# What a convolution tap is queued behind: the last but one stick product named, instead of the last finished attention piece

## The chip, the cores and the metric

The kernel runs on one core of one Trainium2 chip. A core has a tensor engine (PE, with its weight loads listed apart as PEld), a vector engine (DVE), a scalar engine (ACT), GpSimd (POOL) and a queue engine that issues transfers (SP). Each works through its own list of instructions in order, and they wait for one another through semaphores. The metric is the device time of one execution in microseconds; the kernel before took 2762.03 us (median of 3 runs, 2759.02 to 2770.19).

## What is computed

One step of a two-layer encoder, 1024 prompt tokens and 8 x 16 sample tokens (1152 in all), width 1024, in float32. Layer 0 runs two mixers side by side on one projection: stick-breaking attention (8 heads of 64) and a depthwise convolution of 31 taps over 512 channels. Layer 1 is a band attention. Each layer ends with a squared-ReLU MLP.

```python
def stick_breaking(q, k, v, q_pos, k_pos):
    z = jnp.einsum('bqhd,bkhd->bhqk', q, k).astype(jnp.float32) * (HEAD_DIM ** -0.5)
    mask = k_pos[None, :] < q_pos[:, None]
    log_keep = jnp.where(mask, jax.nn.log_sigmoid(-z), 0.0)
    between = lax.cumsum(log_keep, axis=3, reverse=True) - log_keep
    w = jnp.where(mask, jnp.exp(jax.nn.log_sigmoid(z) + between), 0.0)
    return jnp.einsum('bhqk,bkhd->bqhd', w.astype(v.dtype), v)
...
def conv_module(u_ext, dw_w, dw_b, ln_g, ln_b):
    y = lax.conv_general_dilated(
        u_ext, dw_w[:, None, :], window_strides=(1,), padding='VALID',
        dimension_numbers=('NWC', 'WIO', 'NWC'), feature_group_count=CONV_CH) + dw_b
    return jax.nn.silu(layernorm(y, ln_g, ln_b))
```

## The kernel before

**Stages.** Layer 0's mixer fills about the first 560 us of the trace, the rest is its MLP, layer 1 and its MLP. The mixer handles four head pairs p = 0 to 3, one after another. While the attention of pair p runs, the tensor engine also computes the projections of pair p + 1 (`psp`), the convolution's gate and value for later channels (`psg`, `psa`), and the sample attention (`zs`, `so`).

**Attention of a pair.** For each head i (0, 1) and each block t of 256 queries, the two query tiles q = 2t and 2t + 1 go through `one(q)`: scores `z` on PE (L926, L927, L929), two sigmoids on ACT into `sg` and `kp` (L930, L931), then `stick` on DVE: a running product along the keys (the scan, L909) and the product of the sigmoid with it (L911), which writes `sg`, the weights. This last one is the *stick product*. There are 64 of them and 8 for the samples (`sgs`). The weights are turned by PE (`tpa`, L388), copied by ACT (`wa`, L390), multiplied with the values (`ava`, L398), and the two halves are added by DVE at L410 into `cpa`, the finished *attention piece*, of which there are 32. Names carry the pair, the head and the query tile: `sg207` is pair 2, head 0, tile 7.

**Convolution.** The 512 channels are four blocks of 128 (`u0` to `u3`). Each of the 31 taps of a block is two DVE instructions (L734 for the first tap, L737 for the others): 128x1024 elements for the prompt and 128x128 for the samples, added into `y`; the last tap writes back to `u`. The result goes to `cat_d` in DRAM and is read back for the normalisation (`yl`, L1017) while pair 3 runs.

**What sets the order.** The kernel names its instructions in one program order: lists of steps are merged by planned tensor time, and the taps are spread between them by planned vector time (`level`). A scheduler of the framework then orders each engine's own list by what it expects to be ready. A tap depends on little, so it could be placed far ahead of the attention's vector work. L731 holds it back: `tc.issue_after(x)` orders what is named in the block behind instruction x in x's engine list. It adds no semaphore, as both are on DVE. `prior` holds x, and while it is empty (before the first piece) the taps are free.

## Time and profile before

| | |
|---|---|
| median of 3 runs | 2762.03 us (2759.02 to 2770.19) |
| the profiled execution | 2761.51 us, of which the span of its instructions is 2759.7 us |
| instructions in the profile | 50582 |
| DVE taps (L734, L737) | 248, the last starts at 409.7 us |
| stick products (L911) | 72, from 108.6 us to 537.7 us |

The page's first part gives each engine's busy time; a view by windows gives the same for chosen stretches with the granted tensor clock; the view of waits sums what an engine stood idle for, by the instruction that released it; the timeline lists instructions with their start, their duration and, in brackets, the idle time ahead of them and who ended it. All times are counted from the start of the span. DVE instructions overlap slightly at their ends, so what one costs its queue is the distance from its start to the next start.

### The profile page before, as it was taken

Reading aid. Unit: us, or ns where it says so; the run is one execution under the profiler, and the core shown is the slowest. Engines: PE = TensorE matmul, PEld = TensorE weight load, DVE = VectorE, ACT = ScalarE, POOL = GpSimd, SP = SyncE. Lnnn points to the kernel's source line nnn. Section 1 sums busy time; section 2 is a strip of 40 time slices with the busy share of each in tenths; the row PEclk is TensorE's granted clock in tenths of the full one; section 3 lists DMA queues with packets and bytes.
Section 4 is the critical chain, followed back from the end, with each engine's and each line's share of the span. In section 5 each row is a group of like instructions: output and inputs, shape, how many; then the busy total and the mean of one; then the engine's idle time right before and its main releaser. Section 6 shows DMA issues by size and latency. Waiting matters only on the chain.

```text
span 2759.7 us, 50582 instructions
## 1 busy us (share of the span) xinstructions
PE 2681.8 (97%) x19362; PEld 2556.6 (93%) x19362; DVE 2093.9 (76%) x4117; ACT 1388.9 (50%) x2906; POOL 329.4 (12%) x599
## 2 busy tenths in 40 slices
PE   8999998999999999999999999998999999999998
PEld 8987775799999999999999999997999999999998
DVE  8999997888777755758577777778787777647577
ACT  5344456755555543435355555556555555434344
POOL 1000101041111100000011111110221111100001
PEclk9999998999999999999999999999999999999999
DMA  4434446454343377435444444446533343674344
GB/s 157 125 107 145 128 144 201 149 168 139 137 144 142 141 266 248 123 103 167 148 138 139 140 137 133 138 133 222 184 130 137 140 144 139 237 256 136 98 124 144
DMA packets 173203, 422.90 MB, mean 153 GB/s; under 512 B 25968, under 2 KB 53808, under 8 KB 170912
## 3 DMA queue, kind: packets, MB, share of 16 engines
q1 hardware_dynamic: 135696, 288.38, 33.3%
q0 software_dynamic: 37120, 131.27, 13.9%
q8 instruction: 152, 2.49, 0.4%
q14 instruction: 91, 0.75, 0.1%
q10 hardware_dynamic: 144, 0.02, 0.0%
HBM read 289.60 MB, written 117.34 MB: 147 GB/s over the span
## 4 chain that ended last, share of the span: by engine, by line
PE 82%; DVE 10%; ACT 3%; DMA 2%; issue 2%; SPq 0%; DVEq 0%; ACTq 0%; POOLq 0%
PE pd L1692 25%; PE um L1463 25%; PE psc L225 10%; PE psp L225 5%; PE avc L469 2%; PE psoa L225 2%; PE tpc L457 2%; DVE y L737 1%; DVE kp L909 1%; PE f L225 1%; PE zs L570 1%; PE zc L1203 1%; PE psob L225 1%; PE zc L1204 1%; PE ava L398 1%
## 5 line engine op out<-in xcount | busy, mean ns | idle before, releaser
L225 PE MATMUL psc<-h,hl_wc 128*128 128x384 f32 x1728 | 327.2, 339 | 0.0
L225 PEld LDWEIGHTS psc<-h,hl_wc 128*128 128x128 f32 x1728 | 296.8, 188 | 13.3 <-issue 10.9
L1463 PE MATMUL um<-sl,hl_m 128*128 128x288 f32 x1548 | 241.7, 297 | 0.0
L1463 PEld LDWEIGHTS um<-sl,hl_m 128*128 128x128 f32 x1548 | 219.2, 190 | 0.0
L1692 PE MATMUL pd<-tm,hl_wd 128*128 128x288 f32 x1584 | 214.7, 294 | 0.0
L1692 PEld LDWEIGHTS pd<-tm,hl_wd 128*128 128x128 f32 x1584 | 211.2, 189 | 0.0
L737 DVE SCALAR_TENSOR_TENSOR y<-u,dw,y 128x1024 f32<-128x1024 f32 (+1 forms) x232 | 177.5, 807 | 0.5
L225 PE MATMUL psp<-h,hl_wi 128*128 128x384 f32 x864 | 165.2, 343 | 0.0
L1470 ACT ACTIVATE hdm<-hdm 128x288 f32<-128x288 f32 x192 | 84.7, 442 | 156.5 <-DVE hdm L1469 154.9
L225 PEld LDWEIGHTS psp<-h,hl_wi 128*128 128x128 f32 x864 | 149.8, 190 | 7.6 <-issue 7.2
L186 DVE TENSOR_TENSOR tm<-xr,tm 128x576 fp32r<-128x576 f32 (+1 forms) x120 | 85.9, 716 | 93.1 <-ACT tm L185 93.0
L185 ACT ACTIVATE tm<-xr 128x576 fp32r<-128x576 f32 (+1 forms) x120 | 77.6, 647 | 94.4 <-PE pd L1692 76.2
L1463 PE MATMUL um<-sl,hl 128*128 128x288 f32 x756 | 119.1, 296 | 0.0
L1170 ACT ACTIVATE s<-s,mxc 128x640 f32<-128x640 f32 (+4 forms) x128 | 88.8, 694 | 59.6 <-DVE mxc L1167 58.0
L1692 PE MATMUL pd<-th,hl_wd 128*128 128x288 f32 x792 | 113.9, 297 | 3.7 <-DVE th L186 3.5
L1692 PEld LDWEIGHTS pd<-th,hl_wd 128*128 128x128 f32 x792 | 108.4, 190 | 4.6 <-DVE th L186 4.0
L1692 PE MATMUL pd<-xr,hl_wd 128*128 128x288 f32 x792 | 112.2, 295 | 0.0
L1692 PEld LDWEIGHTS pd<-xr,hl_wd 128*128 128x128 f32 x792 | 107.8, 189 | 0.0
L1463 PEld LDWEIGHTS um<-sl,hl 128*128 128x128 f32 x756 | 106.4, 188 | 0.8
L1692 PE MATMUL pd<-tm,hl 128*128 128x288 f32 x768 | 104.9, 295 | 0.0
L1692 PEld LDWEIGHTS pd<-tm,hl 128*128 128x128 f32 x768 | 103.1, 188 | 0.0
L185 ACT ACTIVATE whc<-tpc 128x512 fp32r<-128x512 f32 (+1 forms) x144 | 72.4, 523 | 46.5 <-PE tpc L457 45.6
(526 smaller groups left out, 6651.4 us busy)
## 6 DMA issues: line engine op xcount, KB each, us to landing
xr<-hb_d SPq DMA_DIRECT2D x208, 288.0 KB, 3.0
xr<-in_w_up_dram SPq DMA_DIRECT2D x64, 512.0 KB, 4.3
hb_d<-hdm POOLq DMA_DIRECT2D x96, 288.0 KB, 2.4
hb_d<-t POOLq DMA_DIRECT2D x96, 288.0 KB, 2.4
wm<-in_w_down_dram SPq DMA_DIRECT2D x64, 256.0 KB, 4.1
st_wd<-in_w_down_dram SPq DMA_DIRECT2D x64, 256.0 KB, 3.6
st_wc<-in_w_in_c_dram SPq DMA_DIRECT2D x44, 256.0 KB, 2.9
xm_d<-xo POOLq DMA_DIRECT2D x16, 576.0 KB, 3.6
```

The source lines that it names most:

```text
L185: ACT(hi, src, AF.Copy)
L186: return tt(lo, src, f(hi), ALU.subtract)
L225: mm(ps()[:, :G], hl[:, a, at:at + P], act[g][k // 4][b][:, k % 4, :], start=n == 0, stop=n == len(todo) - 1)
L398: mm(st["av"][64 * m:64 * m + 64, o0:o0 + n], vs[:, j, i], st["w"][gi][:, c0:c0 + n], start=gi == 0, stop=gi == last)
L457: nc.tensor.transpose(tp[:, c0 + q * P:c0 + (q + 1) * P], blocks.get(j, tile_q), ident)
L469: mm(st["av"][:, o0:o0 + n], vs[:, j, i].rearrange("p a d -> p (a d)"), src[:, c0:c0 + n], start=st["done"] == 0, stop=st["done"] == nmm - 1)
L570: mm(box["z"][at // 512][own, at % 512:at % 512 + kw], qb[:, own], k[:, b * kw:b * kw + kw], start=True, stop=True)
L737: stt(src if j == CW - 1 else dst, src, wj, dst, ALU.mult, ALU.add)
L1170: ACT(s[:, :n], s[:, :n], AF.Exp, bias=mx, scale=-1.0, accum_out=tot)
L1463: mm(banks[b, n][:, :TQ], w[:, a, c * P:c * P + P], combo(key, c)[:, h, n * TQ:n * TQ + TQ], start=k < 3 and c == 0 and i == 0, stop=c == ...
L1470: ACT(y, y, AF.Relu)
L1692: mm(ps, w[:, a, m * P:m * P + P], b[:, h, (n - ns[0]) * TQ:(n - ns[0]) * TQ + TQ], start=first and s == 0, stop=j == NJ - 1 and s == 2, s ...
```

## The change

A list `sticks` collects every stick product as it is named. After each one, `prior["weights"]` is set to the last but one of them (to the first, while there is only one). `finish` no longer sets it. So a tap stands behind the stick product named before the latest one, and no longer behind the latest finished piece. Taps named before the first stick product are free, as before they were until the first piece.

```diff
@@ -185,7 +185,7 @@
-    prior = {}
+    prior, sticks = {}, []
 
@@ -407,7 +407,7 @@
-            prior["weights"] = tt(piece[own, one:], av[0:64, one:256], tmp[own, one:], ALU.add)
+            tt(piece[own, one:], av[0:64, one:256], tmp[own, one:], ALU.add)
             cat.put(piece, own, t * 256, 256)
 
@@ -908,7 +908,8 @@
                 nc.vector.tensor_tensor_scan(keep[:, 0:n][:, ::-1], keep[:, 0:n][:, ::-1],
                                              ones[:, 0:1].to_broadcast([P, n]), 1.0, ALU.mult, ALU.mult)
-                tt(w[:, 0:n - 1], w[:, 0:n - 1], keep[:, 1:n], ALU.mult)
+                sticks.append(tt(w[:, 0:n - 1], w[:, 0:n - 1], keep[:, 1:n], ALU.mult))
+                prior["weights"] = sticks[-min(len(sticks), 2)]
```

The instructions are the same ones in both programs. Lines behind L910 are counted one higher in the new kernel. On DVE 232 instructions get another rank in the engine's list, 101 of them tap instructions; the last that is moved starts at 411.7 us in the trace of before, and behind it the lists agree. On PE one group of transposes and two matmuls are moved by a few places.

First place, DVE in pair 0, where the convolution's value `u2` is taken out of PSUM (L717), the sample scores are masked (`zn001`) and half a weight chunk is split (`hl_wi11_0`). Before:

```order
L717 TENSOR_TENSOR u2_1415<-psa21_1652,u2_1415 128x384
L737 SCALAR_TENSOR_TENSOR y1_1239<-u1_389,dw_77,y1_1239 128x1024
L953 TENSOR_TENSOR zn001_1720<-zn001_1720,masks_82 128x128
L737 SCALAR_TENSOR_TENSOR y1_1239<-u1_389,dw_77,y1_1239 128x128
L737 SCALAR_TENSOR_TENSOR y1_1239<-u1_389,dw_77,y1_1239 128x1024
L737 SCALAR_TENSOR_TENSOR y1_1239<-u1_389,dw_77,y1_1239 128x128
L186 TENSOR_TENSOR hl_wi11_0_1776<-st_wi11_0_1774,hl_wi11_0_1776 128x512
```

Now:

```order
L717 TENSOR_TENSOR u2_1415<-psa21_1652,u2_1415 128x384
L954 TENSOR_TENSOR zn001_1720<-zn001_1720,masks_82 128x128
L186 TENSOR_TENSOR hl_wi11_0_1776<-st_wi11_0_1774,hl_wi11_0_1776 128x512
L909 SCALAR_TENSOR_TENSOR kp011_1711<-kp011_1711,ones_74 128x256
L911 TENSOR_TENSOR sg011_1710<-sg011_1710,kp011_1711 128x255
L737 SCALAR_TENSOR_TENSOR y1_1239<-u1_389,dw_77,y1_1239 128x1024
L909 SCALAR_TENSOR_TENSOR kps01_1724<-kps01_1724,ones_74 128x1152
```

The four tap instructions (two taps) between `u2` and the split have gone behind the stick product `sg011`.

Second place, DVE at the start of pair 1, around `sg101`. Before:

```order
L909 SCALAR_TENSOR_TENSOR kps10_2450<-kps10_2450,ones_74 128x1152
L186 TENSOR_TENSOR hl_wi14_1_2501<-st_wi14_1_2499,hl_wi14_1_2501 128x512
L911 TENSOR_TENSOR sgs10_2449<-sgs10_2449,kps10_2450 128x1151
L909 SCALAR_TENSOR_TENSOR kp101_2472<-kp101_2472,ones_74 128x256
L737 SCALAR_TENSOR_TENSOR y2_2281<-u2_1415,dw_77,y2_2281 128x1024
L911 TENSOR_TENSOR sg101_2471<-sg101_2471,kp101_2472 128x255
```

Now:

```order
L909 SCALAR_TENSOR_TENSOR kps10_2450<-kps10_2450,ones_74 128x1152
L909 SCALAR_TENSOR_TENSOR kp101_2472<-kp101_2472,ones_74 128x256
L911 TENSOR_TENSOR sgs10_2449<-sgs10_2449,kps10_2450 128x1151
L911 TENSOR_TENSOR sg101_2471<-sg101_2471,kp101_2472 128x255
L186 TENSOR_TENSOR hl_wi14_1_2501<-st_wi14_1_2499,hl_wi14_1_2501 128x512
```

`sg101` has the half tap and the weight split behind it instead of ahead.

Third place, DVE towards the end of pair 2, around `sg207`; `q0` (L353) and `l0` (L351) prepare the queries and keys of pair 3. Before:

```order
L911 TENSOR_TENSOR sgs21_3946<-sgs21_3946,kps21_3947 128x1151
L737 SCALAR_TENSOR_TENSOR y3_3216<-u3_2561,dw_77,y3_3216 128x128
L353 SCALAR_TENSOR_TENSOR q0_741<-sq03_3559,q0_741 64x1024
L909 SCALAR_TENSOR_TENSOR kp207_3974<-kp207_3974,ones_74 128x1024
L640 COPY cs02_4038<-sq020_4036 64x64
L911 TENSOR_TENSOR sg207_3973<-sg207_3973,kp207_3974 128x1023
```

Now:

```order
L911 TENSOR_TENSOR sgs21_3946<-sgs21_3946,kps21_3947 128x1151
L737 SCALAR_TENSOR_TENSOR y3_3216<-u3_2561,dw_77,y3_3216 128x1024
L737 SCALAR_TENSOR_TENSOR y3_3216<-u3_2561,dw_77,y3_3216 128x128
L737 SCALAR_TENSOR_TENSOR y3_3216<-u3_2561,dw_77,y3_3216 128x1024
L909 SCALAR_TENSOR_TENSOR kp207_3974<-kp207_3974,ones_74 128x1024
L737 SCALAR_TENSOR_TENSOR y3_3216<-u3_2561,dw_77,y3_3216 128x128
L911 TENSOR_TENSOR sg207_3973<-sg207_3973,kp207_3974 128x1023
```

The same taps stand ahead of `sg207` in both (some of them nearer to it now), but `q0` and one of the copies have gone behind it, `q0` together with `l0` by some 15 instructions.

## The prediction

> **What bounds the kernel now.** I read the page first, then the mixer by windows, then what the tensor engine waits for there.

> ```profile
> span 2759.7 us, 50582 instructions
> PE 2681.8 (97%) x19362; PEld 2556.6 (93%) x19362; DVE 2093.9 (76%) x4117; ACT 1388.9 (50%) x2906; POOL 329.4 (12%) x599
> ```

> Over the whole span PE is the bound. The windows (PE, PEld, DVE, ACT, POOL, then granted clock) split the mixer where the taps end:

> ```profile
> 150.00:400.00 250.00, 234.95 (x1772) 195.34 (x1772) 244.03 (x326) 119.39 (x279) 24.56 (x43) 0.99 0.44 132
> 400.00:560.00 160.00, 143.22 (x958) 108.43 (x957) 129.82 (x224) 108.75 (x239) 17.07 (x31) 0.94 0.52 169
> ```

> From 150 to 400 us DVE is busy 98% and PE 94%: two nearly full queues that hold each other up. Moving taps inside this stretch takes no work out of it. The one kind of wait that leads PE's list there:

> ```profile
> PE tpa L388 <- DVE sg L911: 12.3, 7, 3.3
> ```

> That is 12.3 of PE's 250 - 234.95 = 15.05 us of idle time: seven times a transpose waits for a stick product; the rest is two waits for `u`. The timeline of PE gives six of the seven (the other, near 279.6, is what is left, 0.9 us) and the longer wait for `u`:

> ```profile
> 155.95 0.55 PE L388 MATMUL tpa<-ident,sg 128*128 128x128 f32 x3 [1.23 <-DVE sg L911]
> ...
> 164.93 2.38 PE L225 MATMUL psa<-h,hl_wi 128*128 128x384 f32 x12 [1.62 <-DVE u L717]
> ...
> 218.41 0.77 PE L388 MATMUL tpa<-ident,sg 128*128 128x128 f32 x5 [3.23 <-DVE sg L911]
> ...
> 244.71 0.41 PE L388 MATMUL tpa<-ident,sg 128*128 128x128 f32 x2 [1.07 <-DVE sg L911]
> ...
> 335.50 0.77 PE L388 MATMUL tpa<-ident,sg 128*128 128x128 f32 x5 [3.29 <-DVE sg L911]
> ...
> 375.00 0.99 PE L388 MATMUL tpa<-ident,sg 128*128 128x128 f32 x7 [0.83 <-DVE sg L911]
> ...
> 391.99 0.98 PE L388 MATMUL tpa<-ident,sg 128*128 128x128 f32 x7 [1.73 <-DVE sg L911]
> ```

> The chain of waits, cut to 100 to 420 us, shows which taps really stand ahead of such a wait:

> ```profile
> 147.60 3.02 DVE y L737 x5
> ...
> 160.03 4.38 DVE y L737 x6
> ...
> 322.45 4.38 DVE y L737 x6
> ```

> These are the taps ahead of the wait at 155.95, of the one at 164.93 and of the longest one, at 335.50. In the new list they stand where they stood. This is why I expect little.

> **The change, part by part.** It adds and removes no instruction, transfer or semaphore; a product comes earlier or later by the sum of what was moved across it. Because DVE hardly idles there, that sum is the shift.

> *Products that are waited for, unmoved.* Ahead of `sg017` (218.41), `sg107` (near 279.6) and `sg117` (335.50) the list holds the same instructions: shift 0, and these waits hold 3.23 + 0.9 + 3.29 = 7.4 of the 12.3 us.

> *A loss of DVE time at the first place.* DVE and, last, ACT in the trace of before:

> ```profile
> 134.97 0.56 DVE L704 TENSOR_TENSOR u<-u,rh 128x384 f32<-128x384 f32 x1 [0.64 <-ACT u L703]
> ...
> 164.33 0.55 DVE L717 TENSOR_TENSOR u<-psa,u 128x384 f32<-128x384 f32 x1
> 164.80 1.27 DVE L737 SCALAR_TENSOR_TENSOR y<-u,dw,y 128x1024 f32<-128x1024 f32 x1
> 165.99 0.29 DVE L953 TENSOR_TENSOR zn<-zn,masks 128x128 f32<-128x128 f32 x1
> 166.19 1.80 DVE L737 SCALAR_TENSOR_TENSOR y<-u,dw,y 128x128 f32<-128x128 f32 x3
> 168.01 0.69 DVE L186 TENSOR_TENSOR hl_wi<-st_wi,hl_wi 128x512 fp32r<-128x512 f32 x1
> ```

> ```profile
> 167.35 0.63 ACT L185 ACTIVATE hl_wi<-st_wi 128x512 fp32r<-128x512 f32 x1 [0.75 <-PE psa L225]
> ```

> The split at 168.01 needs ACT's half of it, which waits for the twelve `psa` matmuls, which wait for `u` at 164.33. From `u` to the split is 168.01 - 164.33 = 3.68 us whatever DVE does between. Before, the taps filled it. Now only `u` (0.47, to the next start) and the mask (0.20) are left: DVE stands 3.68 - 0.67 = 3.01 us. The taps still have to be done, so all that follows is 3.01 us later, less what comes back. The wait of 0.64 us at 134.97 now has a tap and a half ahead of it and goes: 2.37. Another goes since DVE comes late to it, 0.39 us at 182.50; and the next, 0.46 us at 252.63, by the same reason:

> ```profile
> 182.50 0.28 DVE L410 TENSOR_TENSOR cpa<-ava,ata 64x128 f32<-64x128 f32 x1 [0.39 <-PE z L927]
> ...
> 252.63 0.28 DVE L410 TENSOR_TENSOR cpa<-ava,ata 64x128 f32<-64x128 f32 x1 [0.46 <-ACT cpa L409]
> ```

> DVE's lag is 1.98 us at 218 and 1.52 us from 253 on. Waits of DVE for PE between them are no relief, as PE is late by as much. A query split, 1.22 us as in the row at 387.13 below, goes ahead of `sg007`: the wait at 155.95 grows to 2.45, and the one at 164.93, which PE then reaches later, shrinks from 1.62 to 0.40; sum 0.

> Bounds of the 3.01: nothing, if ACT and PE come earlier than I think, up to all of it. I take 3.01, as all three links are in the rows.

> *Gains.* `sg101`: a half tap and a weight split leave from ahead of it.

> ```profile
> 240.51 0.67 DVE L186 TENSOR_TENSOR hl_wi<-st_wi,hl_wi 128x512 fp32r<-128x512 f32 x1
> 241.10 1.35 DVE L911 TENSOR_TENSOR sgs<-sgs,kps 128x1151 f32<-128x1151 f32 x1
> ...
> 242.97 1.26 DVE L737 SCALAR_TENSOR_TENSOR y<-u,dw,y 128x1024 f32<-128x1024 f32 x1
> 244.14 0.42 DVE L911 TENSOR_TENSOR sg<-sg,kp 128x255 f32<-128x255 f32 x1
> ```

> 0.59 + 1.17 = 1.76 us earlier, against a lag of 1.98: the product is 0.22 late, PE itself 1.98 - 1.07 = 0.91. PE goes on 0.91 us late, until the waits for DVE near 279.6 and at 335.50 put it back to DVE's 1.52. So this gain is swallowed.

> `sg205` loses one tap from ahead of it, `sg207` the query split and a copy:

> ```profile
> 370.89 1.28 DVE L737 SCALAR_TENSOR_TENSOR y<-u,dw,y 128x1024 f32<-128x1024 f32 x1
> 372.09 1.75 DVE L909 TENSOR_TENSOR_SCAN kp<-kp,ones 128x768 f32<-128x768 f32 x1
> 373.75 0.33 DVE L737 SCALAR_TENSOR_TENSOR y<-u,dw,y 128x128 f32<-128x128 f32 x1
> 374.00 0.95 DVE L911 TENSOR_TENSOR sg<-sg,kp 128x767 f32<-128x767 f32 x1
> ```

> ```profile
> 387.13 1.22 DVE L353 SCALAR_TENSOR_TENSOR q<-sq,q 64x1024 fp32r<-64x1024 f32 x1
> ...
> 390.59 0.19 DVE L640 COPY cs<-sq 64x64 f32<-64x64 f32 x1
> 390.70 1.23 DVE L911 TENSOR_TENSOR sg<-sg,kp 128x1023 f32<-128x1023 f32 x1
> ```

> 1.20 + 0.25 = 1.45 for the first: 0.07 late, and PE, 1.52 late but 0.83 us of wait shorter, is 0.69 late. 1.22 + 0.11 = 1.33 for the second: 1.52 - 1.33 = 0.19 us late. PE's 0.69 is inside the old wait of 1.73, so PE leaves 391.99 with 0.19 us, and behind it the lists agree from 411.7 on.

> *Moved preparations.* `q0` and `l0` of pair 3 end some 11 to 17 us later, near 405, and the first output-weight split 14 us later, near 407. PE uses them here:

> ```profile
> 433.38 0.99 PE L225 MATMUL psoa<-cat,hl_wo0a 128*128 128x384 f32 x2
> ...
> 437.25 2.85 PE L1023 MATMUL mu<-yl,ones 128*128 128x384 f32 x8
> ...
> 447.90 0.33 PE L926 MATMUL z<-k,q 128*128 128x128 f32 x1
> ```

> Some 26 and 40 us of cover; without it they would cost what they are late. The last tap ends about 2.6 us later (two scans and a product, 0.9, 1.2 and 0.5 us, go ahead of it), near 412.6, and what POOL issues behind it to bring the convolution back (`yl`) moves with it; its first reader, `mu` at 437.25, is 25 us off. POOL and SP change a few places in their lists by this, with no instruction of PE near them. I cost all of it at 0.

> **Sum**: 3.01 - 0.64 - 0.39 - 0.46 - 1.33 = +0.19 us. The profiled execution took 2761.51 us (span 2759.7 and 1.8 around it), so 2761.7; it lies 0.5 below the median, so a median is **2762.2 us**.

> **The clock.** Two waits of the same length end differently:

> ```profile
> 210.00:220.00 10.00, 6.77 (x42) 5.87 (x42) 9.81 (x12) 4.27 (x10) 4.18 (x7) 1.00 0.70 184
> 330.00:340.00 10.00, 6.71 (x35) 6.07 (x38) 9.85 (x14) 1.55 (x4) 2.17 (x4) 0.83 0.51 145
> ```

> The 3.23 us wait kept the full clock, the 3.29 us one cost 0.17 of ten microseconds, 1.7 us of tensor time. A longer wait can cost as much at 218, and a shift can save it at 335. [...]

> **Rivals.**
> *Starved and throttled (slower).* DVE's 3.01 us come through whole, as PE finds no slack, and the wait at 218 grows to over 5 us and loses clock: 1.7 there and 1.7 in one more wait of the stretch from 400 on, whose 0.94 shows how easily it is lost. 3.01 + 3.4 = +6.4: 2767.9 us. For it: the three links above. Against: the gain at `sg207`. It decides once the lag at 390 is over 1.33 us.
> *The waits go (faster).* If ordering DVE by sticks freed all seven waits: 2761.5 - 12.3 = 2749.2. Against it: 7.4 of the 12.3 have shift 0, and the two engines stay full.
> *Nothing at all.* The shifts cancel in the waits and ACT fills the hole: 2761.5 us, not to be told from my forecast.

> **Chances.** Forecast 0.60, nothing at all 0.14, starved 0.19, faster 0.07. The own bounds of the sum are -0.64 - 1.33 - 1.7 = -3.7 (no hole, a clock window saved) and 3.01 + 1.7 = +4.7, that is 2757.8 to 2766.2; with the 11 us over which the three runs of before lie (down 3, up 8 from their median) and part of the starved case the range is 2755 to 2771. About 0.5%, 13.8 us, is what a measurement of this kernel can tell from no change. No case reaches that; for a mechanism that I don't see I leave 0.03 faster and 0.05 slower, so the same is 0.92.

> **What would show it.** Right: DVE idle for about 3 us ahead of a split near 164 to 168 us, waits of some 5.2 us at 218 and 3.3 at 335, none left at 244.7 and 375.0, about 1.2 near 392, and 560 us reached within 2 us of before. Wrong in the first step if DVE shows no such hole; wrong in the sum if PE's idle time in 150 to 400 us falls by over 5 us, or if the stretch behind 411 us, whose lists agree, changes by more than the clock does.

## The result, and the profile after

The changed kernel takes 2767.12 us (median of 22 runs, 2765.39 to 2769.95), the kernel before beside it 2762.41 us (22 runs, 2757.56 to 2770.19). The ratio is 1.0016 with a 95% interval of 1.0010 to 1.0023: 4.7 us slower at the medians, 2.8 to 6.4 us by the interval. A second, later comparison gave 1.0015 (1.0006 to 1.0023). The loss is small, but it is there. The profiled execution took 2769.12 us. One run of the kernel before, 3236 us at a granted clock of 0.751, is left out of the means and ratios below.

The page of the changed kernel, busy times:

```profile
span 2767.3 us, 50587 instructions
PE 2686.0 (97%) x19362; PEld 2556.2 (92%) x19362; DVE 2094.6 (76%) x4117; ACT 1388.6 (50%) x2906; POOL 329.6 (12%) x599
```

VectorE's work is the same (2094.6 us, 2093.9 before). TensorE's 19362 matmuls are busy 4.2 us longer (2686.0 us, 2681.8 before): the same work at a lower clock (0.989 over the profiled execution, 0.991 before). The windows of the changed kernel say where (PE, PEld, DVE, ACT, POOL, then granted clock; from 400 to 560 us the clock is 0.94 as before):

```profile
150.00:400.00 250.00, 233.95 (x1694) 194.02 (x1694) 234.36 (x309) 116.40 (x272) 23.52 (x41) 0.96 0.42 127
560.00:2755.00 2195.00, 2164.75 (x15826) 2121.53 (x15825) 1582.46 (x3336) 1086.54 (x2239) 270.07 (x482) 1.00 0.48 156
```

In the stretch from 150 to 400 us PE finishes 1694 matmuls where it finished 1772, at a clock of 0.96 instead of 0.99, and DVE is busy 234.4 us instead of 244.0: it now stands 9.7 us longer there. What PE waits for in that stretch (us in total, times, longest):

```profile
PE tpa L388 <- DVE sg L911: 11.4, 5, 5.2
PE psa L225 <- DVE u L717: 3.1, 1, 3.1
```

The waits for stick products are fewer and hardly shorter in sum (11.4 us, 12.3 before). A wait for the sum `u` has grown to 3.1 us; in the kernel before it was this one:

```profile
271.74 2.38 PE L225 MATMUL psa<-h,hl_wi 128*128 128x384 f32 x12 [1.13 <-DVE u L717]
```

PE's timeline of the changed kernel:

```profile
157.20 0.55 PE L388 MATMUL tpa<-ident,sg 128*128 128x128 f32 x3 [1.61 <-DVE sg L911]
221.84 1.54 PE L388 MATMUL tpa<-ident,sg 128*128 128x128 f32 x6 [5.24 <-DVE sg L911]
278.47 4.21 PE L225 MATMUL psa<-h,hl_wi 128*128 128x384 f32 x12 [3.08 <-DVE u L717]
325.04 0.55 PE L388 MATMUL tpa<-ident,sg 128*128 128x128 f32 x3 [0.94 <-DVE sg L911]
344.57 0.87 PE L388 MATMUL tpa<-ident,sg 128*128 128x128 f32 x6 [3.35 <-DVE sg L911]
401.27 0.98 PE L388 MATMUL tpa<-ident,sg 128*128 128x128 f32 x7 [0.82 <-DVE sg L911]
```

The wait at 218.41 (3.23 us before) is now 5.24 us, and behind it six transposes take 1.54 us where five took 0.77 before. Behind the wait at 278.47 twelve matmuls take 4.21 us instead of some 2.4. DVE's timeline shows where it stands idle:

```profile
164.20 0.55 DVE L717 TENSOR_TENSOR u<-psa,u 128x384 f32<-128x384 f32 x1
166.18 0.30 DVE L954 TENSOR_TENSOR zn<-zn,masks 128x128 f32<-128x128 f32 x1 [1.43 <-PE zn L575]
168.95 0.69 DVE L186 TENSOR_TENSOR hl_wi<-st_wi,hl_wi 128x512 fp32r<-128x512 f32 x1 [2.47 <-ACT hl_wi L185]
...
239.66 0.42 DVE L410 TENSOR_TENSOR cpa<-ava,ata 64x256 f32<-64x256 f32 x1 [2.26 <-ACT ata L406]
243.85 2.56 DVE L909 TENSOR_TENSOR_SCAN kps<-kps,ones 128x1152 f32<-128x1152 f32 x1 [0.85 <-ACT kps L959]
258.57 0.56 DVE L704 TENSOR_TENSOR u<-u,rh 128x384 f32<-128x384 f32 x1 [0.41 <-ACT u L703]
259.88 1.49 DVE L909 TENSOR_TENSOR_SCAN kp<-kp,ones 128x640 f32<-128x640 f32 x1 [0.74 <-ACT kp L932]
...
287.97 0.42 DVE L410 TENSOR_TENSOR cpa<-ava,ata 64x256 f32<-64x256 f32 x1 [1.93 <-ACT ata L406]
```

The predicted hole is at 164 to 169 us, 1.43 + 2.47 = 3.90 us wide. Four more stand behind it up to 290 us: 239.66 (2.26 us, 0.59 before), 243.85, 258 to 260, 287.97. By the last stick product of head pair 2 (`sg217`, at 430.9 us before, at 440.4 now) the changed execution is 9.5 us behind the profiled execution of before.

**The clock, slice by slice.** The windows below are cut where the granted clock changes, or a whole multiple of 3.41 us ahead of such a place (333.00 only nearly). First the kernel before, around its wait of 3.23 us at 218.41 and its wait of 3.29 us at 335.50:

```profile
213.47:216.88 3.41, 1.71 (x10) 1.38 (x8) 3.35 (x3) 0.08 (x1) 1.14 (x3) 1.00 0.90 215
216.88:220.30 3.42, 1.89 (x14) 1.90 (x14) 3.33 (x7) 1.10 (x2) 1.25 (x3) 1.00 0.85 196
220.30:223.71 3.41, 3.41 (x31) 1.81 (x30) 3.41 (x6) 0.37 (x1) 0.00 (x0) 1.00 0.69 197
333.00:336.35 3.35, 0.85 (x7) 0.85 (x8) 3.26 (x6) 0.27 (x1) 0.35 (x1) 1.00 0.67 222
336.35:339.76 3.41, 3.41 (x13) 3.27 (x11) 3.41 (x6) 0.82 (x2) 0.74 (x2) 0.50 0.33 96
```

Then the changed kernel, around its waits at 221.84 and 278.47:

```profile
216.27:219.68 3.41, 0.33 (x2) 0.01 (x1) 3.35 (x3) 0.00 (x0) 1.79 (x4) 1.00 0.91 218
219.68:226.51 6.83, 4.67 (x16) 4.23 (x17) 6.74 (x12) 1.19 (x2) 1.25 (x3) 0.50 0.83 221
274.29:277.70 3.41, 1.09 (x8) 0.72 (x6) 3.41 (x6) 2.67 (x5) 0.00 (x0) 1.00 0.55 217
277.70:284.53 6.83, 6.06 (x19) 4.87 (x20) 6.80 (x8) 0.68 (x2) 0.00 (x0) 0.50 0.00 0
```

From 60 to 560 us these two executions have 5 and 8 stretches at 0.50, each 3.41 or 6.83 us long, and within one execution they start whole multiples of 3.413 us apart. I call 3.41 us, counted from such a start, a slice. Behind the slices in which PE was busy for 0.85, 0.33 and 1.09 us the clock was 0.50. The kernel before's wait at 218 lay across two slices, with 1.71 us of work in one and 1.89 in the other, and the clock stayed at 1.00. The prediction was made from that execution.

### The profile page after: what moved, and what is told of

Its sections match the earlier page's. It is cut to its first block, busy times and chain, and to the rows that moved or that the text cites. A ratio compares the mean times of both kernels' runs of the same rounds, so it can differ in the third digit from the quotient of the medians.

```text
span 2767.3 us, 50587 instructions
## 1 busy us (share of the span) xinstructions
PE 2686.0 (97%) x19362; PEld 2556.2 (92%) x19362; DVE 2094.6 (76%) x4117; ACT 1388.6 (50%) x2906; POOL 329.6 (12%) x599
## 3 DMA queue, kind: packets, MB, share of 16 engines
q8 instruction: 152, 2.49, 0.4%
## 4 chain that ended last, share of the span: by engine, by line
PE 79%; DVE 13%; ACT 3%; issue 3%; DMA 2%; SPq 0%; DVEq 0%; POOL 0%; ACTq 0%; POOLq 0%
PE um L1464 25%; PE pd L1693 24%; PE psc L225 10%; PE psp L225 3%; DVE y L737 2%; PE psob L225 2%; PE avc L469 2%; DVE kp L909 2%; PE psoa L225 2%; PE tpc L457 2%; PE f L225 1%; PE zc L1204 1%; PE zs L570 1%; PE zc L1205 1%; DVE sg L911 1%
## 5 line engine op out<-in xcount | busy, mean ns | idle before, releaser
L225 PE MATMUL psc<-h,hl_wc 128*128 128x384 f32 x1728 | 327.2, 340 | 0.0
L225 PEld LDWEIGHTS psc<-h,hl_wc 128*128 128x128 f32 x1728 | 296.9, 188 | 13.3 <-issue 10.9
L737 DVE SCALAR_TENSOR_TENSOR y<-u,dw,y 128x1024 f32<-128x1024 f32 (+1 forms) x232 | 178.2, 812 | 0.6
L225 PE MATMUL psp<-h,hl_wi 128*128 128x384 f32 x864 | 166.9, 346 | 0.0
L186 DVE TENSOR_TENSOR tm<-xr,tm 128x576 fp32r<-128x576 f32 (+1 forms) x120 | 86.0, 718 | 97.4 <-ACT tm L185 97.2
L225 PEld LDWEIGHTS psp<-h,hl_wi 128*128 128x128 f32 x864 | 151.0, 191 | 7.7 <-issue 6.8
L185 ACT ACTIVATE tm<-xr 128x576 fp32r<-128x576 f32 (+1 forms) x120 | 77.6, 647 | 97.7 <-PE pd L1693 74.9
L185 ACT ACTIVATE whc<-tpc 128x512 fp32r<-128x512 f32 (+1 forms) x144 | 72.3, 522 | 46.5 <-PE tpc L457 44.8
```

Source lines behind the costliest of these rows:

```text
L185: ACT(hi, src, AF.Copy)
L186: return tt(lo, src, f(hi), ALU.subtract)
L225: mm(ps()[:, :G], hl[:, a, at:at + P], act[g][k // 4][b][:, k % 4, :], start=n == 0, stop=n == len(todo) - 1)
L737: stt(src if j == CW - 1 else dst, src, wj, dst, ALU.mult, ALU.add)
```

## The experiments

The table gives four numbers for each kernel. The ratio is over its runs and the runs of the kernel before beside them. The clock is the granted clock of a whole execution, as a mean over the same runs (for the kernel before over the 88 runs beside all later kernels). The mixer part is read from the one profiled execution: from the start of the first score matmul (`z<-k,q`, near 104 us) to the start of `sg217`; the rest is from there to the end of the span.

| kernel | ratio (95%) | clock | mixer part, us | rest, us |
|---|---|---|---|---|
| before | 1 | 0.9904 | 326.9 | 2328.8 |
| changed | 1.0016 (1.0010 to 1.0023) | 0.9897 | 335.9 | 2326.9 |
| changed, again | 1.0015 (1.0006 to 1.0023) | 0.9896 | 333.9 | 2322.6 |
| new rule in pair 0 only | 1.0007 (0.9997 to 1.0016) | 0.9896 | 332.4 | 2323.8 |
| new rule in pairs 1 and 2 only | 1.0009 (1.0000 to 1.0018) | 0.9896 | 332.3 | 2324.8 |
| hole alone | 1.0006 (0.9994 to 1.0017) | 0.9899 | 330.1 | 2329.1 |
| hole alone, again | 1.0004 (0.9993 to 1.0015) | 0.9902 | 330.2 | 2325.1 |
| hole filled | 1.0017 (1.0006 to 1.0027) | 0.9896 | 335.0 | 2327.5 |
| before, PE kept busy at 218 | 0.9989 (0.9978 to 0.9999) | 0.9914 | 326.4 | 2327.0 |
| the same, again | 0.9987 (0.9978 to 0.9996) | 0.9915 | 326.4 | 2326.1 |
| changed, PE kept busy at 222 | 1.0019 (1.0010 to 1.0028) | 0.9899 | 332.6 | 2327.8 |
| the same, again | 1.0018 (1.0010 to 1.0027) | 0.9899 | 332.2 | 2328.6 |

0.0001 of clock is 0.28 us of tensor time over 2760 us, so one half-speed slice of 3.41 us (1.7 us of tensor time) is 0.0006. The clock's means are uncertain by 0.0002 to 0.0004. The rest scatters by 6.5 us from one execution to the next, though the instruction lists in it stand in one order for all of these kernels.

### Which half of the change costs the time

The first theory was that the hole in VectorE's list at 164 to 169 us costs the time and the clock behind it doubles the price; the rival, that the products moved in the stages of head pairs 1 and 2 do. Both kernels keep both rules and choose by the tap's number:

```diff
-                with tc.issue_after(prior["weights"].ins) if prior else ExitStack():
+                first = prior.get("weights" if c * CW + j < 62 else "piece")
+                with tc.issue_after(first.ins) if first else ExitStack():
```

Here "weights" is the last but one stick product and "piece" the last finished attention piece; the second kernel has `>= 62`.

> The new rule holds for the taps up to number 61 (those that stand in the stage of head pair 0 and ahead of it), the old rule for all later taps. Theory (the hole in VectorE at about 166 to 171 us is what costs, and the longer tensor waits behind it lose the tensor clock): nearly the whole loss of the change is here, +3 to +5 us against the kernel before, with a tensor wait of about 5 us near 222 us and half-speed tensor work behind it. Rival (the products and preparations that were moved in the stages of pairs 1 and 2 cost the time): within 1 us of the kernel before.

> The converse: old rule up to tap 61, new rule from tap 62 on, so that the stage of head pair 0 is as in the kernel before. Theory (hole in pair 0): within 1.5 us of the kernel before, rather faster (-1 us), since the waits of 0.9 to 1.7 us at 271 to 392 us shrink and no hole is made. Rival (pairs 1 and 2): +3 to +5 us.

Measured: 1.0007 is +1.9 us (-0.8 to +4.4), 1.0009 is +2.5 us (0 to +5.0). The two halves add up to 4.4 us, close to the +4.7 of the whole, and by these values neither carries it alone. Neither the theory as I had it nor its rival is borne out, though both intervals reach into the +3 to +5 us that one of them asked for.

The second kernel showed something better. Up to `sg017` its VectorE list is that of the kernel before, and so is its wait, 3.22 us. PE's timeline of that kernel, and the windows cut at the slices:

```profile
218.73 1.75 PE L388 MATMUL tpa<-ident,sg 128*128 128x128 f32 x7 [3.22 <-DVE sg L912]
275.84 3.92 PE L225 MATMUL psa<-h,hl_wi 128*128 128x384 f32 x12 [3.06 <-DVE u L717]
```

```profile
214.52:217.93 3.41, 0.99 (x6) 0.67 (x4) 3.38 (x4) 0.00 (x0) 0.42 (x1) 1.00 0.86 249
217.93:224.76 6.83, 6.03 (x27) 5.29 (x27) 6.74 (x12) 1.20 (x2) 1.25 (x3) 0.50 0.57 153
272.54:275.95 3.41, 0.35 (x4) 0.12 (x2) 3.41 (x6) 3.23 (x6) 0.00 (x0) 1.00 0.39 161
275.95:279.36 3.41, 3.41 (x11) 3.41 (x12) 3.41 (x5) 0.00 (x0) 0.00 (x0) 0.50 0.00 0
```

The same wait, but the slice ahead holds 0.99 us of work instead of 1.71, and behind it 6.83 us run at 0.50. VectorE then stands and waits for what PE delivers late: 0.72 us for `psp`, and 2.49 us ahead of `cpa` (0.59 before), which needs `ata`, ACT's copy of PE's `ava`. Its stick product `sg100` comes 3.05 us later than before, where `sg017` was 0.32 us later. Up to there the lists of PE and VectorE are those of the kernel before. So 2.7 us of this execution, at this place, are the clock alone, after a wait that the change did not touch.

What the new rule itself does in pair 1 is a second hole, of the kind that I found in pair 0. In the kernel before, the tap instruction at 252.84 us stands between the finished piece `cpa` and the sum `u`:

```profile
252.84 1.27 DVE L737 SCALAR_TENSOR_TENSOR y<-u,dw,y 128x1024 f32<-128x1024 f32 x1
254.03 0.55 DVE L704 TENSOR_TENSOR u<-u,rh 128x384 f32<-128x384 f32 x1
254.50 1.48 DVE L909 TENSOR_TENSOR_SCAN kp<-kp,ones 128x640 f32<-128x640 f32 x1
```

With the new rule it goes ahead of the two, and VectorE stands (kernel with the new rule in pairs 1 and 2):

```profile
253.35 1.53 DVE L738 SCALAR_TENSOR_TENSOR y<-u,dw,y 128x1024 f32<-128x1024 f32 x2
254.81 0.55 DVE L702 TENSOR_TENSOR u<-psg,rh 128x384 f32<-128x384 f32 x1
255.28 0.27 DVE L410 TENSOR_TENSOR cpa<-ava,ata 64x128 f32<-64x128 f32 x1
255.95 0.56 DVE L704 TENSOR_TENSOR u<-u,rh 128x384 f32<-128x384 f32 x1 [0.40 <-ACT u L703]
257.25 1.49 DVE L910 TENSOR_TENSOR_SCAN kp<-kp,ones 128x640 f32<-128x640 f32 x1 [0.75 <-ACT kp L933]
```

0.40 + 0.75 = 1.15 us are lost; the wait of 0.46 us at 252.63 is gone. PE's wait for `u` behind it is 3.06 us here, 3.08 in the changed kernel, and 1.87 us in the two kernels that keep the old order in pair 1 and have a late VectorE (new rule in pair 0 only; hole alone). Behind the wait of 3.06 to 3.08 us the twelve `psa` matmuls took 3.92 us here, 4.21 in the changed kernel, 3.77 and 3.72 in the two traces of the changed kernel with PE kept busy at 222, where the kernel before, after 1.13 us of wait, took 2.38. Not always: in the second trace of the changed kernel they took 2.36 us behind the same wait:

```profile
278.94 2.36 PE L225 MATMUL psa<-h,hl_wi 128*128 128x384 f32 x12 [3.06 <-DVE u L717]
```

### The hole by itself

Two kernels move only taps 15 and 16 of the second channel block (numbers 46 and 47), whose four instructions stood in the hole. The first is the kernel before with the new rule for these two alone, the second the changed kernel with the old rule for these two:

```diff
+                first = prior.get("weights" if c * CW + j in (46, 47) else "piece")
```

```diff
+                first = prior.get("weights" if c * CW + j not in (46, 47) else "piece")
```

> The kernel before with the new rule for two taps alone, 15 and 16 of the second channel block (tap numbers 46 and 47), those that the change moves from between the sum u2<-psa21 and the split hl_wi11_0 to behind the stick product sg011. Theory: this alone makes the VectorE hole of 3 to 4 us, the tensor wait near 220 us grows from 3.2 to 5 us or more, and tensor work at half speed follows it: +3 to +5 us. Rival (the hole, but no price of the clock): +2 to +3 us at most, with no more half-speed slices than the kernel before has. Rival (pairs 1 and 2 are the cause): within 1 us.

> The changed kernel with the old rule for taps 46 and 47 alone, which puts the four tap instructions back into the hole; all other taps follow the new rule. Theory: the loss is gone, within 1.5 us of the kernel before, and the tensor wait near 220 us is 3.3 us or shorter. Rival (pairs 1 and 2): as slow as the changed kernel, +3 to +5 us.

The first makes the hole as predicted. VectorE's timeline of the kernel with the hole alone:

```profile
165.06 0.55 DVE L717 TENSOR_TENSOR u<-psa,u 128x384 f32<-128x384 f32 x1
165.53 0.28 DVE L955 TENSOR_TENSOR zn<-zn,masks 128x128 f32<-128x128 f32 x1
168.72 0.69 DVE L186 TENSOR_TENSOR hl_wi<-st_wi,hl_wi 128x512 fp32r<-128x512 f32 x1 [2.90 <-ACT hl_wi L185]
```

and PE's, the wait that it lengthens:

```profile
221.61 1.54 PE L388 MATMUL tpa<-ident,sg 128*128 128x128 f32 x6 [5.24 <-DVE sg L912]
```

2.90 us of hole for 3.01 predicted, and 5.24 us of wait. Yet its time is +1.7 us (-1.7 to +4.7), and again +1.1 us (-1.9 to +4.1): less than the +3 to +5 expected, and not to be told from zero. What was expected of the second comparison stands further below.

The second fills the hole and wins nothing: 1.0017, as slow as the changed kernel. Its wait is no shorter:

```profile
223.10 1.54 PE L388 MATMUL tpa<-ident,sg 128*128 128x128 f32 x6 [5.37 <-DVE sg L912]
```

The hole was 1.2 us here instead of 3.9, but with these two taps back, other taps slid ahead of `sg017`: 127 tap instructions stand ahead of it, 124 in the kernels before and changed. An idle time ahead of the product, or work ahead of it, makes it as late. The expectation was wrong: I had asked only what stood in the hole, and not what the list would put in front of `sg017` instead.

### Keeping TensorE busy in the wait

If the clock has a price, busy work in the wait must win time, though the data come no sooner. These kernels write idle transposes of the identity into the bank of the waiting group, behind the 12 `psp` matmuls and ahead of the group's real transposes:

```diff
+                    with tc.issue_after(m.ins):
+                        for r in range({'a013': 24}[name]):
+                            m = nc.tensor.transpose(tp[:, r % 4 * P:r % 4 * P + P], ident, ident)
```

Here `m` is the last of the twelve matmuls, and the group's real transposes are issued behind the last idle one; the changed kernel gets 44 of them. The scheduler answers with a few more moved rows: 21 instructions on VectorE, all behind `sg017`, get another rank for the kernel before, 20 for the changed one.

> The changed kernel with 44 idle transposes (about 4.8 us) in its 5.24 us wait near 222 us. Theory: no half-speed slice near 222 us; two half slices (3.4 us of tensor time at most, 1.7 at least) are won, so the changed kernel's +4.7 us over the kernel before falls to +1 to +3 us; the wait for psa31 near 278 us (3.1 us) and its half slice stay. Rival (lag of VectorE alone, no price of the clock): it stays at +4 to +5 us.

> The kernel before with the idle transposes in its wait near 218 us, again: 1.47 such slices for 2.43, so by the clock alone -1.6 us; measured first -3.0 [-6.1, -0.3]. Rival (no price of the clock): 0.

> The changed kernel with the idle transposes in its wait near 222 us, again: 1.88 slices for 3.41, so 2.6 us below the changed kernel of the same call, +0.8 us against the kernel before. Rival (the lag of VectorE is the whole price, the clock gives nothing here): as the changed kernel, which is what the first run showed (+5.2 us [2.8, 7.7]).

> The changed kernel again, beside the next three on one chip. A sum over the stretch from 90 to 415 us of the profiled executions: tensor waits 15.4 us before, 17.1 us changed; 3.41 us slices in which TensorE is busy less than half, counted over all phases of the grid, 2.43 before, 3.41 changed, each worth 1.7 us of tensor time. Theory (waits plus clock): +1.7 + 1.7 = +3.4 us; measured first +4.7 [2.8, 6.3].

> The hole alone, again: tensor waits 17.5 us for 15.4, slices 3.56 for 2.43, so +2.1 + 1.9 = +4.0 us by waits plus clock; +2.1 us by the waits alone. Measured first +1.8 [-1.7, +4.7].

The kernel before with PE kept busy, PE's timeline and the windows:

```profile
217.82 2.78 PE L393 MATMUL tpa<-ident 128*128 128x128 f32 x24
220.44 0.27 PE L397 MATMUL tpa<-ident,sg 128*128 128x128 f32 x1
221.29 0.98 PE L397 MATMUL tpa<-ident,sg 128*128 128x128 f32 x7 [0.58 <-DVE sg L922]
```

```profile
216.60:223.40 6.80, 6.22 (x48) 5.95 (x48) 6.67 (x9) 1.09 (x2) 2.16 (x5) 1.00 0.88 203
```

It is faster than the kernel before: -3.0 us (-6.1 to -0.3), and again -3.6 us (-6.1 to -1.1). The moved rows are not the reason as far as the traces tell: its mixer part is 326.4 us twice, and that of the kernel before, in the one execution that kept the clock at 218, 326.9. The clock is: 0.9914 and 0.9915 over the runs for 0.9904, which is 2.9 us of tensor time, about the time won. No kernel with the moved rows and without the idle transposes was run. The 2.9 us are 1.7 half-speed slices a run, by which I infer (an estimate) that the kernel before usually loses the clock at this wait, and that its profiled execution was a lucky one. No second trace of the kernel before was taken that would show it; what shows it in one execution is the kernel with the new rule in pairs 1 and 2, whose lists and wait are the same up to there and whose clock fell to 0.50. It would also say why the hole alone costs so little: behind its wait of 5.24 us six transposes take 1.54 us, as in the changed kernel at half speed, but by this estimate the wait of 3.23 us had mostly lost the clock already.

The changed kernel with PE kept busy is a miss. Its trace holds what was expected, 44 idle transposes, a wait of 0.89 us and the full clock (1.00 from 215.90 to 226.10 us):

```profile
216.86 4.97 PE L393 MATMUL tpa<-ident 128*128 128x128 f32 x44
222.83 0.98 PE L397 MATMUL tpa<-ident,sg 128*128 128x128 f32 x7 [0.89 <-DVE sg L922]
```

Its mixer part is 332.6 and 332.2 us, shorter than the changed kernel's 335.9 and 333.9. But its time is +5.2 and +5.0 us over the kernel before, no better than the changed kernel's +4.4 and +4.1. Over the runs the clock rose by only 0.0003 (0.9896 to 0.9899), 0.8 us of tensor time and half of one slice, where the changed kernel's trace has two slices (6.83 us) at 0.50 behind its wait of 5.24 us. In the two traces the rest took 2328 us instead of 2323 to 2327, within the scatter that all kernels show there. Why a won mixer wins no time here is open.

The single runs hold a hint. In the kernels that keep the old rule in pairs 1 and 2 (the kernel before, new rule in pair 0 only, hole alone, PE kept busy at 218; 145 runs), runs of one kernel with 0.001 more clock were 2.0 us shorter, with a standard error of 0.14. In those with the new rule there (79 runs) it was 0.6 us (0.25), in the changed kernel itself 0.35 us (0.37). So with the new rule in pairs 1 and 2 a better clock went with little time. This is a comparison between runs, and what holds the time there was not tested.

Against the sums of waits and slices that the repeats were given: the changed kernel +4.1 for +3.4 us, the hole alone +1.1 for +4.0, PE kept busy -3.6 for -1.6 in the kernel before and +5.0 for +0.8 in the changed one. A sum of waits plus half-speed slices does not give these times.

### Three waits at once

> The kernel before with idle transposes in the three longest tensor waits for the last stick product of a head pair's second half: 24 in group a013 (wait 3.23 us near 218 us), 24 in a113 (3.29 us near 335 us), 22 in a213 (3.18 us near 421 us). Theory: three half-speed slices of 1.7 us tensor time are kept, -3 to -5 us against the kernel before. Rival: within 0.7 us, or slower.

> The changed kernel with 44, 24 and 22 idle transposes in the same three waits. Theory: 5 to 7 us less than the changed kernel, that is 0 to 2 us below the kernel before; the difference to the kernel before with the same three waits filled is the hole's lag (1.7 us more wait in all) and the half slice behind the 3.1 us wait at 278 us, +2 to +4 us. Rival: +4 to +5 us as the changed kernel.

Measured 1.0034 (1.0021 to 1.0047) and 1.0063 (1.0050 to 1.0076), slower than either kernel. The rows of the first say that it doesn't test the theory:

```profile
334.92 0.90 PE L397 MATMUL tpa<-ident,sg 128*128 128x128 f32 x3 [3.27 <-DVE sg L922]
335.61 5.11 PE L393 MATMUL tpa<-ident 128*128 128x128 f32 x23
...
444.73 1.60 PE L225 MATMUL psoa<-cat,hl_wo0a 128*128 128x384 f32 x3 [5.24 <-ACT cat L185]
446.12 4.06 PE L393 MATMUL tpa<-ident 128*128 128x128 f32 x19
```

The wait near 335 is as long as ever. The idle transposes came behind it, at half speed (23 in 5.11 us, where 24 took 2.78 above), and cost 5.1 us; those of the third group came behind output matmuls that wait 5.24 us for ACT, and cost 4.1 us. In the second kernel they stand behind the two waits as well. Busy work behind a wait is only more work.

## Why the prediction was right or wrong

The time, 2767.1 us, lies inside the range, and the change is within 0.5%, as was given 0.92. The range of 16 us held the forecast and two of its three rivals, so this says little about the mechanism. The likeliest case, 2762.2 us, is wrong: its sum of +0.19 us measured +4.7. What came was the rival called *Starved and throttled*, at 2767.9 us, to which I gave 0.19; its number is close, its mechanism only in part: the hole came and the wait at 218 lost the clock, but the clock of the stretch from 400 on, where it saw the second loss, did not change (0.94), and the second hole and the second wait for `u` are not in it.

*The hole at the first place: right.* 2.90 us where it was made alone, 3.90 in the changed kernel's first trace and 0.58 + 2.47 = 3.05 in its second, 3.01 predicted. "3.68 us whatever DVE does" was wrong in the first trace: from `u` to the split were 168.95 - 164.20 = 4.75 us, as PE's clock had fallen to 0.50 behind the wait at 157.20 (from 158.24 to 161.65 us). The predicted lag of 1.98 us at 218 was near too: counted from the first score matmul, `sg017` came 3.1 us later than in the kernel before in the first trace and 2.2 us in the second. The waits were predicted as 2.45, 0.40 and some 5.2 us, and were 1.61, none and 5.24.

*The terms -0.64 and -0.39 came.* Neither wait is left in DVE's timeline of the changed kernel, as predicted.

*The term -0.46 has the wrong sign.* The wait at 252.63 (0.46 us) went, and 0.41 + 0.74 = 1.15 us of new waits stand at 258 to 260, where the moved tap had stood: 0.69 us lost in place of 0.46 won. This is the step of the sum that failed: I checked one place for a hole and took the waits at all others as something that could only shrink.

*The term -1.33 drowned.* The product `sg207` does lose what stood ahead of it, and the wait there fell from 1.73 to 0.82 us. But by then the lag was 9 us in that execution, not 1.52, and two waits of PE at 325.04 (0.94 us) and 385.53 (1.24) are new.

*The wait for `u` at 271.74 was left out.* I walked the waits for stick products and the first wait for `u`, and not the second, 1.13 us. It grew to 3.08 us, the largest change behind 222, and it lost the clock in the first trace of the changed kernel but not in the second (4.21 and 2.36 us for the twelve matmuls behind it).

*The clock was put at zero in the sum.* The prediction saw that two waits of the same length ended differently and left open why. The full clock at 218, taken for the kernel's, was that of one execution. What differed in the traces was the work in the slice ahead: 0.85, 0.99 and 1.09 us of 3.41 were followed by 0.50, 1.71 us by 1.00. A wait of 3.2 to 3.3 us was followed by one slice at 0.50 (at 335 in the kernel before) or two (at 218 with the new rule in pairs 1 and 2), 1.7 or 3.4 us of tensor time, and behind the wait of 3.06 to 3.08 us the twelve matmuls took 3.72 to 4.21 us in four of the five traces above and 2.36 in one. The wait of 5.24 us was followed by two (6.83 us), where *Starved and throttled* had 1.7 us, one slice; against the kernel before it would add less, if that mostly pays at that place already. The 1.7 us that the lower bound of the prediction took as saved at 335 did not come: behind the wait of 3.35 us at 344.57 the changed kernel's clock was 0.50 too (from 345.97 to 349.38 us).

*Right.* 3.3 us at 335 (3.35), no wait left at 244.7, 0.82 near 392 for "about 1.2", and the preparations cost nothing that a row shows. At 375.0, where none was to be left, 0.25 of 0.83 us is, at 383.75. Wrong by its own test: 560 us was to be reached within 2 us of before, and the lists from 431 on run 9.5 us behind the profiled execution of before. The two rivals that expected no loss, *The waits go* and *Nothing at all*, fell: the sum of waits for stick products only went from 12.3 to 11.4 us.

*The division.* By the mean clock over the runs, 0.9904 to 0.9897 and 0.9896, at most some 2.1 us of the +4.7 and +4.1 are lost clock (0.00075 of 2760 us), if TensorE was the bound in all of it. By the 2.0 us for 0.001 between single runs it would be 1.5, by the 0.35 us of the changed kernel's own runs 0.3; the rest would be lag. That is worked out, not shown by a run: the two halves of the change cost about 2 us each, with intervals that reach to zero, and the idle transposes, which win 3 us in the kernel before, win nothing in the changed one. What they run into there stays open.

## What to carry to other kernels

When work is moved away from between two dependent steps on another engine, look at every place where it stood, not only at the first, and ask what then stands in front of the next product that is waited for; a hole and an early filler delay it alike. One profiled execution shows one outcome: behind the same wait of 3.2 us the clock stayed at 1.00 in one trace here and fell to 0.50 in another. Price such a wait both ways, look whether runs with more clock are shorter at all, and compare the length of a stage between two markers rather than the total. Where a wait can't be shortened, busy work of the right length inside it can keep the clock (here 1.00 with 24 idle transposes in the kernel before, for -3.0 and -3.6 us, and 1.00 with 44 in the changed one, for nothing), and behind it, it only cost (5.1 and 4.1 us).

## What the runs showed of the hardware that I had not expected

In these traces the clock fell behind slices in which TensorE had worked, up to 1.80 us of 3.41. From 60 to 560 us the profiled executions of the kernel before and of the changed kernel have 12 slices at full speed that were busy for 0.33 to 1.62 us, and each was followed by one at 0.50. Of the next four, the slice with 1.80 us (changed, at 154.82) was followed by 0.50, those with 1.71, 1.79 and 1.89 us (before, at 213.47, 162.27 and 216.88) by 1.00; behind all that were busy for 1.94 us or more it stayed at 1.00. Behind the half-speed slices with 0.94 to 3.02 us of work came a second one, behind those with 3.06 to 3.41 us the full clock. In the kernel before with PE kept busy at 218, the 24 idle transposes are part of the 6.22 us that PE is busy from 216.60 to 223.40 us, and the clock there was 1.00.
